# Attention with a bias on one core: V landed straight into its ring of 24 heads, late K landed side by side, joined output stores, five output tiles, 24 exponentials on VectorE

## The chip, the core and the metric

The kernel runs on one NeuronCore of a Trainium2 chip. Five engines work side by side, each in the order of its own queue: TensorE (PE, with its weight loads shown as PEld), ScalarE (ACT), VectorE (DVE), GpSimd (POOL) and SyncE (SP). Here SP issues plain DMAs only, and POOL issues only the DMAs that change float32 to bfloat16 on the way, with a one-element copy now and then (tile `tick`) that makes POOL wait until an earlier load has landed. The metric is the device time of one execution in microseconds (us). Before the change it is 231.16 us, the median of three runs (231.0 to 231.25). A change of more than 0.2% (0.46 us) is taken as told from none.

## What is computed

Four batches of eight heads, 1024 queries and 1024 keys of 64 numbers, and one bias of 1024 x 1024 that all 32 heads share:

```python
scores = scale * np.matmul(q, k.transpose(0, 1, 3, 2))
scores = scores + bias
scores_max = np.max(scores, axis=-1, keepdims=True)
attn = np.exp(scores - scores_max) / (np.sum(np.exp(scores - scores_max), axis=-1, keepdims=True) + 1e-8)
return np.matmul(attn, v).astype(np.float32)
```

The kernel leaves the maximum out (scores are small) and gets the sum of a row from a column of ones beside V.

## The kernel before

**Slots.** The 32 heads are 16 pairs, 0 to 15. A head has eight chunks of 128 queries, and one chunk of one head is a slot; 256 slots. A slot has 1024 x 128 scores (transposed) in one of three places in PSUM (`pl`, two banks each), its exponential in an `E` tile, and an output of 128 x 64. For each slot PE runs 16 matmuls of scores (`fill_half`, line 254), ACT one exponential over 128 x 1024 (`exp`, line 268), and PE eight matmuls of E with V (`av`, line 318). A place keeps its scores from one head to the next: the two halves of the contraction add the scores of this head and take away those of the last one, so that the bias is written (line 251) only where a place starts on a new chunk.

**Two groups.** The first seven pairs make slots 0 to 111, the other nine slots 112 to 255. In the first group the 14 heads run over chunks 0 to 2 (slots 0 to 41), then chunks 3 and 4 (42 to 69), then 5 to 7; so the bias chunks 3 and 4 and the rest of q of pairs 0 and 1 (`qrest`) are first used at slots 42 to 48. In the second group every pair takes six slots to begin with: pair 7 starts at slot 112, pair 15 at slot 160.

**Exponentials on DVE.** The slots in `PLAN`, 23 of them, have their exponential made by DVE in five instructions (`d_steps`, lines 285 to 301). 233 remain on ACT, the first of them in two halves.

**Loads.** POOL's order is fixed: bias 1 and 2, then k, q and v of the early pairs (`EARLY` = 7 pairs), among them the rests of q and the bias chunks 3 to 7 last; then from pair 7 on k, q and v of the late pairs (`load`, line 490). `issue` (line 478) puts a `tick` ahead of a load, which waits for the load that was issued four or five loads before (early) or two loads before (late, `LATE` = 2). q of the late pairs is loaded by `beside` (line 137): two DMAs, one for each head of the pair, that write runs of 64 numbers (128 bytes) so that the two heads lie side by side; it is then transposed in eight matmuls (line 191) where the other form takes sixteen (line 195). k of the late pairs takes the other form: one DMA with runs of 1024 bytes. v (`load_v`, line 167) lands the same way in one of three tiles `v16`, and DVE copies it into `vall` (line 508), a ring of 20 heads in which each run of 64 numbers has a one behind it.

**From a load to its first use.** PE transposes (tile `px`), DVE copies out (`ko`, `qo`), DVE negates late q (line 228), and SP copies halves from tile to tile (`ke`, `qe`, line 565).

**Outputs.** Seven slots share one bank of PSUM (`po`). `evac` (line 321) divides on DVE into an `ob` tile, one of three, and gives a store to `of` for each run of neighbouring chunks of one head; SP issues them (line 739), ACT the last.

**The order.** A planner in the kernel walks through its own model of the engines (costs such as `EXP`, `AV`, `ISSUE`, landing times such as `LATE_LOADS`) and emits each engine's instructions in the order that results. `TURNS` and `D_TURNS` are places where a listed candidate is taken rather than the rule's. The model decides only the order; on the chip semaphores hold an instruction until what it needs is there, and what stands behind it in its queue waits with it.

Of the kernel before, what the change touches and what calls it, by code (L numbers as in the profile page):

```python
# [9 lines left out]
BF = mybir.dt.bfloat16  # L10
# [6 lines left out]
def kernel(  # L17
# [13 lines left out]
    nc = tc.nc  # L31
    B, H, S, D = q.shape
# [15 lines left out]
    SPLIT, EARLY = 2, 7  # L48
    RING = 9
    LANDS = 5  # L50
    NE = 16
    VL = 3
    C0 = 3

    SIDE, SIDES = 3, 1
# [1 line left out]
    consts = ctx.enter_context(tc.tile_pool(name="consts", bufs=1))  # L57
    land = ctx.enter_context(tc.tile_pool(name="land", bufs=LANDS))
    side = ctx.enter_context(tc.tile_pool(name="side", bufs=SIDES))
    vland = ctx.enter_context(tc.tile_pool(name="vland", bufs=VL))  # L60
    kq = ctx.enter_context(tc.tile_pool(name="kq", bufs=RING))
    ep = ctx.enter_context(tc.tile_pool(name="ep", bufs=NE))
    op = ctx.enter_context(tc.tile_pool(name="op", bufs=3))
    dp = ctx.enter_context(tc.tile_pool(name="dp", bufs=2))
    dy = ctx.enter_context(tc.tile_pool(name="dy", bufs=3))
    de = ctx.enter_context(tc.tile_pool(name="de", bufs=2))
# [14 lines left out]
    zeros = ep.tile([P, NCH, P], BF, name="E")[:, :4].rearrange("p c q -> p (c q)")  # L81
    braw = consts.tile([P, NCH, S], BF)

    VR = 20
    vall = consts.tile([P, VR, NCH, D1], BF)

    b0f = dp.tile([P, S], F32, name="df")
# [35 lines left out]
    for s, x in enumerate(slots):  # L123
# [2 lines left out]


    dslots = set()
    PLAN = (46, 52, 56, 73, 84, 87, 97, 107, 120, 128, 137, 149, 160, 167, 170, 182, 188, 194, 208, 214, 226,
            230, 240)  # L130

    raws, lands, arrs = {}, {}, {}


    BESIDE = (0,)

    def beside(pr, x):

# [26 lines left out]
        return braw[:1, c, S - 1:]  # L165

    def load_v(pr):
        lands[pr, "v"] = vland.tile([P, 2, NCH, D], BF, name="v16")
        nc.gpsimd.dma_start(out=lands[pr, "v"].rearrange("p t c d -> p t (c d)"),  # L169
                            in_=vf[pr].rearrange("p t c d -> p t (c d)"))  # L170
        return lands[pr, "v"][:1, 1, NCH - 1, D - 1:]

    def arrays(pr):
        if pr not in arrs:
# [134 lines left out]
    def av(group, b, tag):  # L309
# [6 lines left out]
        for kc in range(NCH):  # L316
            for i, s in enumerate(group):
                nc.tensor.matmul(po[:, j + i, :], etile[s][:, kc, :], vall[:, slots[s][2] % VR, kc, :],  # L318
                                 start=j + i + kc == 0, stop=kc == NCH - 1, skip_group_check=True)

    def evac(b):

        po, units = bank[b]
        n = len(units)
        rs = small.tile([P, 7, 1], F32, name="rs")
        nc.vector.reciprocal(rs[:, :n, :], po[:, :n, D:D1])  # L326
        ob = olast if n == 1 else op.tile([P, 7, D], F32, name="ob")
        nc.vector.tensor_tensor(ob[:, :n, :], po[:, :n, :D], rs[:, :n, :].to_broadcast([P, n, D]), op=ALU.mult)  # L328
        stores = []

        j = 0
        while j < n:
            x, c, h, start = slots[units[j]]
            i = j + 1
            while i < n and slots[units[i]][1:3] == (c + i - j, h):
                i += 1
            stores.append((of[:, h, c:c + i - j, :], ob[:, j:i, :]))
            j = i
        return stores

    with tc.manual_schedule():

# [54 lines left out]
        double(0, 1, 0, NCH, 1, nc.vector)  # L397
        double(0, 0, 0, C0, 1, nc.vector)

        FILL, BIAS, AV = 452, 500, 264  # L400
        L_PE, L_FILL, L_ACT, L_DVE = 195, 256, 265, 140
        EXP = 904
        ISSUE, COPY = 70, 7000
        T0 = 8600.0
        bias_at = {0: T0, 1: T0, 2: 9600}
        raw_at = {(1, 1, 0): 10800, (1, 0, 0): 11500, (2, 1, 0): 12700, (2, 0, 0): 14300}
        v_at, vland_at = {}, {0: 16300}
        t_dma = 15500
        DUE = (78, 86, 137, 98, 82, 97, 114, 84, 144)
        t_pe, t_act, t_dve, t_pool = 9300.0, 9900.0, 9600.0, 9000  # L410
        filled, used = {0: T0}, {0: 9900 + L_ACT}
        av_done = {}
        e_at = {0: used[0]}
        x_free = {"xa": T0, "xb": T0}
# [37 lines left out]
        DEP = 115  # L452
        MARGIN = 160
        VSLACK = 800
        WINDOW = 4

        side_q = [x[:3] for x in pieces if SIDE <= x[0] < EARLY and x[2] == 0]
        side_open, side_at = [], {}
# [19 lines left out]
        def issue(at, cost, depth, load, pr, *a):  # L478

            nonlocal t_dma  # L480
            if 0 < depth <= len(flight):
                what, t = flight[-depth]
                nc.gpsimd.tensor_copy(tick[:], what)  # L483
                at = max(at, t + 100)
            at = pool(at, 750)
            t_dma = max(t_dma + cost, at + 2200 + cost)
            flight.append((load(pr, *a), t_dma + 200))
            return t_dma + 200
# [8 lines left out]
        def next_v(t):  # L497

            while loads_v and not any(x[2] // 2 == loads_v[0] - VR // 2 and y not in av_done for y, x in enumerate(slots)):
                if loads_v[0] - VL not in v_at:  # L500
                    break
                p = loads_v.pop(0)
                vland_at[p] = issue(t, 1600, LATE + (p > 12), load_v, p) + 2000
                move_v(p)

        def move_v(pr):
            def run(t2):
                nc.vector.tensor_copy(vall[:, 2 * pr % VR:2 * pr % VR + 2, :, :D], lands[pr, "v"][:])
                v_at[pr] = t2 + 430 + L_DVE
                next_v(v_at[pr])  # L510
            dve_q.append((vland_at[pr] + VSLACK * (pr >= EARLY), 0.3, 430, run))


        def early(kind, pr):
            nonlocal t_dma
# [207 lines left out]
        def pool(at, cost=0):  # L723
            nonlocal t_pool
            t_pool = max(t_pool, at) + cost
            return t_pool
# [49 lines left out]
        def pe_pick():  # L776
            c = pe_cands()
            if not c:
                return None
            if done_pe in TURNS:  # L780
                c.sort(key=lambda x: (x[0], x[3], x[4]))
                return c[TURNS[done_pe] % len(c)]
            fills = [x for x in c if x[3] == 0]
            others = [x for x in c if x[3] != 0]
            if others and NE <= next_act < len(acts) and acts[next_act - NE] not in av_done:

                return min(others, key=lambda x: (x[3] != 1, x[0]))
            now = [x for x in fills if x[0] <= t_pe]
            if now:


                short = len([s for s in avq[:NE] if s in e_at]) > NE - 3
                due = [x for x in others if x[3] in ((0.5, 1) if short else (0.5,)) and x[0] <= t_pe]
                if due and act_free() - FILL - L_FILL - MARGIN > t_pe + due[0][1]:
                    return due[0]
                return min(now, key=lambda x: x[4])

            limit = 1e12
            r = [y for y in (fill_ready(z[0]) for z in queue.values() if z and z[0] <= next_fill + WINDOW) if y is not None]
            if r:  # L800
                limit = max(min(r), act_free() - FILL - L_FILL - MARGIN)
            ok = [x for x in others if x[0] + x[1] <= limit]
            return min(ok + fills, key=lambda x: (x[0], x[3])) if ok + fills else None

        def dve_pick():
# [10 lines left out]
            if best[1] >= 3:  # L816
                soon = [x for x in can if x[1] < 3 and x[0] < start + 350]
                if soon:
# [1 line left out]
            return best  # L820

        done_pe, done_dve = 0, 0
        TURNS = {9: 2, 15: 0, 25: 1, 30: 0, 49: 2, 63: 2, 64: 0, 74: 1, 93: 0, 94: 0, 98: 0, 105: 0, 109: 0,
# [3 lines left out]
        D_TURNS = {1: 0, 25: 0, 34: 1, 39: 2, 41: 1, 42: 1, 44: 1, 66: 0, 68: 0, 70: 1, 71: 0, 76: 1, 81: 1,  # L827
                   82: 0, 83: 0, 88: 1, 91: 1, 107: 1, 125: 2, 128: 1, 162: 1, 165: 0, 166: 0, 171: 2, 176: 1,
                   184: 1, 195: 0, 199: 1, 201: 1, 203: 1, 204: 1, 208: 2, 211: 2, 212: 1, 222: 0}

        move_v(0)
        for x in ("k3", "q3", "v1", "k4", "q4", "v2", "k5", "q5", "v3", "k6", "q6", "v4") + tuple(LATE_LOADS):
# [75 lines left out]
```

## Time and profile before

| | before |
|---|---|
| median of three runs | 231.16 us |
| the profiled execution | 231.17 us |
| its span on the core | 229.2 us |
| granted TensorE clock, mean | 0.995 |
| GpSimd busy | 65.1 us |
| software DMA queue (POOL's loads), 30336 packets | 14.06 MB |
| hardware DMA queue (SP's copies and stores), 26560 packets | 14.40 MB |
| output stores | 158 |

The span goes from the first to the last instruction of the core; about 2 us of the time lie outside it. Busy time is the union of an engine's instructions. In a row of the timeline stand the start, the length, the engine, line, operation and tiles, and in brackets how long the engine was idle before it and what ended that. In a row of a DMA queue the share is the time that its packets took, over the time of all 16 DMA engines; an engine with two packets under way at once can bring it over 100%.

### The profile page before, as it was taken

Reading aid. Unit: us, or ns where it says so; the run is one execution under the profiler, and the core shown is the slowest. Engines: PE = TensorE matmul, PEld = TensorE weight load, DVE = VectorE, ACT = ScalarE, POOL = GpSimd, SP = SyncE. Lnnn points to the kernel's source line nnn. Section 1 sums busy time; section 2 is a strip of 40 time slices with the busy share of each in tenths; the row PEclk is TensorE's granted clock in tenths of the full one; section 3 lists DMA queues with packets and bytes.
Section 4 is the critical chain, followed back from the end, with each engine's and each line's share of the span. In section 5 each row is a group of like instructions: output and inputs, shape, how many; then the busy total and the mean of one; then the engine's idle time right before and its main releaser. Section 6 shows DMA issues by size and latency. Waiting matters only on the chain.

```text
span 229.2 us, 10571 instructions
## 1 busy us (share of the span) xinstructions
PE 219.4 (96%) x4607; PEld 208.8 (91%) x4607; DVE 197.0 (86%) x301; ACT 218.1 (95%) x238; POOL 65.1 (28%) x115
## 2 busy tenths in 40 slices
PE   7899989999999999999999999999999999899992
PEld 2789989999999999999899999999999999899991
DVE  2578878629977999999999999999999999999952
ACT  3699999999999999999999999999999999999992
POOL 8816466256455443443224310000000000000000
PEclk9999999999999999999999999999999999999998
DMA  6999999989999999999899994111121102311122
GB/s 195 216 204 215 227 227 186 223 118 110 135 113 179 169 159 184 179 97 178 207 163 243 169 238 113 49 43 43 43 50 39 44 9 66 82 50 40 34 77 75
DMA packets 57373, 29.75 MB, mean 130 GB/s; under 512 B 34864, under 2 KB 53680, under 8 KB 57328
## 3 DMA queue, kind: packets, MB, share of 16 engines
q0 software_dynamic: 30336, 14.06, 49.3%
q1 hardware_dynamic: 26560, 14.40, 23.2%
q8 instruction: 36, 0.59, 1.1%
q10 hardware_dynamic: 432, 0.62, 0.9%
q14 instruction: 9, 0.07, 0.1%
HBM read 29.36 MB, written 8.39 MB: 165 GB/s over the span
## 4 chain that ended last, share of the span: by engine, by line
PE 54%; ACT 14%; DVE 12%; issue 7%; DMA 5%; SPq 5%; DVEq 0%; ACTq 0%
PE pl L254 31%; PE po L318 16%; ACT E L268 14%; SPq L739 5%; DMA out_dram<-ob 3%; PE px L191 3%; PE pl L251 2%; PE px L195 2%; DVE dy L285 2%; DMA df<-in_k_dram 2%; DVE ob L328 2%; DVE df L296 1%; DVE de L301 1%; DVE ko L203 1%; DVE side L222 1%
## 5 line engine op out<-in xcount | busy, mean ns | idle before, releaser
L268 ACT ACTIVATE E<-pl 128x1024 bf16<-128x1024 f32 (+1 forms) x234 | 215.0, 1094 | 2.3 <-PE pl L254 2.0
L318 PE MATMUL po<-vall,E 128*128 128x65 bf16 x1864 | 86.2, 194 | 1.1 <-DVE qo L205 0.4
L254 PE MATMUL pl<-qo,ko 128*128 128x128 bf16 x1024 | 77.0, 219 | 1.2 <-ACT E L268 0.6
L318 PEld LDWEIGHTS <-E 128*128 128x128 bf16 x1864 | 74.0, 98 | 2.0 <-DVE ob L328 0.6
L254 PEld LDWEIGHTS <-ko 128*128 128x128 bf16 x1160 | 69.4, 98 | 4.3 <-issue 1.4
L254 PE MATMUL pl<-qe,ke 128*128 128x128 bf16 x888 | 65.4, 219 | 0.9 <-ACT E L268 0.3
L254 PEld LDWEIGHTS <-ke 128*128 128x128 bf16 x888 | 53.2, 98 | 2.6 <-issue 0.7
L285 DVE TENSOR_SCALAR dy<-pl 128x1024 int32<-128x1024 f32 x23 | 28.0, 1218 | 1.8 <-PE pl L254 1.7
L301 DVE SCALAR_TENSOR_TENSOR de<-dy,df 128x1024 uint16<-128x1024 int32 x23 | 27.9, 1219 | 0.7 <-PE po L318 0.4
L296 DVE SCALAR_TENSOR_TENSOR df<-df 128x1024 f32<-128x1024 f32 x23 | 28.0, 1217 | 0.1
L293 DVE SCALAR_TENSOR_TENSOR df<-df 128x1024 f32<-128x1024 f32 x23 | 27.9, 1217 | 0.1
L328 DVE TENSOR_TENSOR ob<-po,rs 128x448 f32<-128x448 f32 (+4 forms) x40 | 23.3, 583 | 2.6 <-DMA out_dram<-ob 1.1
L142 POOL DMA_DIRECT2D q<-in_q_dram x18 | 16.3, 907 | 4.4 <-PE pl L254 2.7
L326 DVE RECIPROCAL rs<-po 128x7 f32<-128x7 f32 (+5 forms) x41 | 7.9, 192 | 9.9 <-PE po L318 9.8
L290 DVE TENSOR_SCALAR df<-dy 128x1024 f32<-128x1024 uint16 x23 | 15.8, 687 | 0.3
L483 POOL COPY tick<-q 1x1 bf16<-1x1 bf16 x12 | 4.4, 367 | 33.4 <-DMA q<-in_q_dram 33.4
L203 DVE COPY ko<-px 128x1024 bf16<-128x1024 bf16 (+1 forms) x16 | 10.7, 668 | 3.3 <-PE px L195 2.5
L205 DVE TENSOR_SCALAR qo<-px,sgn 128x1024 bf16<-128x1024 bf16 (+2 forms) x18 | 12.3, 683 | 1.2 <-PE px L191 1.0
L169 POOL DMA_DIRECT2D v<-in_v_dram x16 | 11.3, 707 | 2.0 <-DVE df L296 0.3
L251 PE MATMUL pl<-ident,braw 128*128 128x128 bf16 x136 | 11.3, 226 | 0.0
L149 POOL DMA_DIRECT2D k<-in_k_dram x15 | 10.7, 711 | 2.1 <-issue 0.8
L251 PEld LDWEIGHTS <-braw 128*128 128x128 bf16 x136 | 9.9, 148 | 0.0
(58 smaller groups left out, 125.4 us busy)
## 6 DMA issues: line engine op xcount, KB each, us to landing
v<-in_v_dram POOLq DMA_DIRECT2D x16, 256.0 KB, 6.6
k<-in_k_dram POOLq DMA_DIRECT2D x15, 256.0 KB, 5.5
out_dram<-ob SPq DMA_DIRECT2D x33, 96.0 KB, 3.9
out_dram<-ob SPq DMA_DIRECT2D x92, 32.0 KB, 2.6
ke<-ko SPq DMA_DIRECT2D x22, 128.0 KB, 5.5
q<-in_q_dram POOLq DMA_DIRECT2D x18, 128.0 KB, 4.7
qe<-q SPq DMA_DIRECT2D x17, 128.0 KB, 5.0
out_dram<-ob SPq DMA_DIRECT2D x31, 64.0 KB, 2.7
```

Source lines behind the costliest of these rows:

```text
L142: nc.gpsimd.dma_start(out=t[:, :, y, :], in_=(qf, kf)[x][pr][:, y].rearrange("p (c d) -> p c d", d=D))
L203: nc.vector.tensor_copy(t["ko"][:, cs, :], px[:])
L251: nc.tensor.matmul(to, braw[:, c, :].rearrange("p (kp kc) -> p kc kp", kc=NCH)[:, kc, :], ident8[:], start=i == 0, stop=False, skip_group_ ...
L254: nc.tensor.matmul(to, kk[:, kc, :], qq[:, c, :], start=False, stop=True, skip_group_check=True)
L268: nc.scalar.activation(e[:, i:i + n].rearrange("p b x -> p (b x)"), places[slots[s][0]][:, i:i + n].rearrange("p b x -> p (b x)"), ACTF.Ex ...
L285: w.tensor_scalar(t["y"][:], places[slots[s][0]].rearrange("p b x -> p (b x)"), scale * LOG2E * 65536.0, 127.0 * 65536.0, op0=ALU.mult, op ...
L290: w.tensor_scalar(t["f"][:], t["lo"], GU / 65536.0, None, op0=ALU.mult)
L293: w.scalar_tensor_tensor(t["f"][:], t["f"][:], GP, t["f"][:], op0=ALU.add, op1=ALU.mult)
L296: w.scalar_tensor_tensor(t["f"][:], t["f"][:], GQ, t["f"][:], op0=ALU.add, op1=ALU.mult)
L301: w.scalar_tensor_tensor(etile[s].bitcast(U16).rearrange("p c q -> p (c q)"), t["y"][:], 1.0 / 512.0, t["f"][:], op0=ALU.mult, op1=ALU.add)
L318: nc.tensor.matmul(po[:, j + i, :], etile[s][:, kc, :], vall[:, slots[s][2] % VR, kc, :], start=j + i + kc == 0, stop=kc == NCH - 1, skip_ ...
L328: nc.vector.tensor_tensor(ob[:, :n, :], po[:, :n, :D], rs[:, :n, :].to_broadcast([P, n, D]), op=ALU.mult)
```

## The change

- **V in place.** `load_v` writes into `vall` itself, one DMA for each head of the pair, with runs of 64 numbers. The copy on DVE and the `v16` tiles are gone. `vall` has 24 heads in place of 20.
- **Late k side by side.** `BESIDE = (0, 1)`: k of pairs 7 to 15 is loaded as late q is, by two DMAs, and transposed in eight matmuls.
- **Stores joined.** `joined` also puts into one store the same chunk of heads at an equal distance, and takes the longest run first. Five `ob` tiles in place of three.
- **24 DVE slots** in `PLAN`, at other places; 15 `E` tiles in place of 16.
- **The planner**: other model costs (`BIAS` 530, `ISSUE` 420, 1450 for POOL's issue of v and of late q), `GRACE` = 16 (an AV group or a transpose may end 16 ns past its limit), other `DUE`, and empty `TURNS` and `D_TURNS`. A load of v no longer waits for a copy of an earlier one.

```diff
-    NE = 16
-    VL = 3
+    NE = 15
-    op = ctx.enter_context(tc.tile_pool(name="op", bufs=3))
+    op = ctx.enter_context(tc.tile_pool(name="op", bufs=5))
-    VR = 20
+    VR = 24
-    PLAN = (46, 52, 56, 73, 84, 87, 97, 107, 120, 128, 137, 149, 160, 167, 170, 182, 188, 194, 208, 214, 226,
-            230, 240)
+    PLAN = (24, 44, 50, 60, 75, 80, 90, 102, 104, 117, 136, 153, 159, 161, 169, 183, 189, 191, 198, 212, 218,
+            223, 229, 246)
-    BESIDE = (0,)
+    BESIDE = (0, 1)
     def load_v(pr):
-        lands[pr, "v"] = vland.tile([P, 2, NCH, D], BF, name="v16")
-        nc.gpsimd.dma_start(out=lands[pr, "v"].rearrange("p t c d -> p t (c d)"),
-                            in_=vf[pr].rearrange("p t c d -> p t (c d)"))
-        return lands[pr, "v"][:1, 1, NCH - 1, D - 1:]
+        for t in range(2):
+            nc.gpsimd.dma_start(out=vall[:, (2 * pr + t) % VR, :, :D], in_=vf[pr][:, t])
+        return vall[:1, (2 * pr + 1) % VR, NCH - 1, D - 1:D]
+    def joined(units):
+        out, left = [], list(range(len(units)))
+        while left:
+            best = left[:1]
+            for j in left[1:]:
+                run, dj = [left[0], j], j - left[0]
+                dc, dh = (units[j][i] - units[left[0]][i] for i in range(2))
+                if min(dc, dh) < 0 or dc and dh:
+                    continue
+                while run[-1] + dj in left and units[run[-1] + dj] == (units[run[-1]][0] + dc, units[run[-1]][1] + dh):
+                    run.append(run[-1] + dj)
+                best = max(best, run, key=len)
...
-        stores = []
...
+        return [(to, ob[:, js]) for to, js in joined([slots[u][1:3] for u in units])]
-        FILL, BIAS, AV = 452, 500, 264
+        FILL, BIAS, AV = 452, 530, 264
-        ISSUE, COPY = 70, 7000
+        ISSUE, COPY = 420, 7000
-        DUE = (78, 86, 137, 98, 82, 97, 114, 84, 144)
-        t_pe, t_act, t_dve, t_pool = 9300.0, 9900.0, 9600.0, 9000
+        DUE = (63, 123, 126, 134, 73, 76, 102, 62, 96)
+        t_pe, t_act, t_dve, t_pool = 9050.0, 9740.0, 9600.0, 9000
-        WINDOW = 4
+        WINDOW, GRACE = 4, 16
-            at = pool(at, 750)
+            at = pool(at, 1450 if load is load_v or load is load_q and pr >= EARLY else 750)
             while loads_v and not any(x[2] // 2 == loads_v[0] - VR // 2 and y not in av_done for y, x in enumerate(slots)):
-                if loads_v[0] - VL not in v_at:
-                    break
         def move_v(pr):
-            def run(t2):
-                nc.vector.tensor_copy(vall[:, 2 * pr % VR:2 * pr % VR + 2, :, :D], lands[pr, "v"][:])
-                v_at[pr] = t2 + 430 + L_DVE
-                next_v(v_at[pr])
-            dve_q.append((vland_at[pr] + VSLACK * (pr >= EARLY), 0.3, 430, run))
+            v_at[pr] = vland_at[pr] + VSLACK * (pr >= EARLY) + 300
-            ok = [x for x in others if x[0] + x[1] <= limit]
+            ok = [x for x in others if x[0] + x[1] <= limit + GRACE]
-        TURNS = {9: 2, 15: 0, 25: 1, 30: 0, 49: 2, 63: 2, 64: 0, 74: 1, 93: 0, 94: 0, 98: 0, 105: 0, 109: 0,
...
+        TURNS = {}
+        D_TURNS = {}
```

More of the change, by code (lines that the diff above doesn't have):

```diff
@@ L59 @@
     side = ctx.enter_context(tc.tile_pool(name="side", bufs=SIDES))
-    vland = ctx.enter_context(tc.tile_pool(name="vland", bufs=VL))
     kq = ctx.enter_context(tc.tile_pool(name="kq", bufs=RING))
     ep = ctx.enter_context(tc.tile_pool(name="ep", bufs=NE))
-    op = ctx.enter_context(tc.tile_pool(name="op", bufs=3))
+    op = ctx.enter_context(tc.tile_pool(name="op", bufs=5))
     dp = ctx.enter_context(tc.tile_pool(name="dp", bufs=2))
@@ L319, in av @@
                                  start=j + i + kc == 0, stop=kc == NCH - 1, skip_group_check=True)
+    def joined(units):
[10 more added lines that the diff above has]
+                best = max(best, run, key=len)
+            left = [j for j in left if j not in best]
+            (c, h), (c1, h1) = units[best[0]], units[best[-1]]
+            k = len(best) - 1
+            to = of[:, h, c:c1 + 1:max(1, (c1 - c) // max(1, k)), :] if h == h1 else of[:, h:h1 + 1:(h1 - h) // k, c, :]
+            out.append((to, slice(best[0], best[-1] + 1, best[1] - best[0] if k else 1)))
+        return out
     def evac(b):
@@ L328, in evac @@
         nc.vector.tensor_tensor(ob[:, :n, :], po[:, :n, :D], rs[:, :n, :].to_broadcast([P, n, D]), op=ALU.mult)
-        stores = []
[L331 to L339, printed above, removed]
+        return [(to, ob[:, js]) for to, js in joined([slots[u][1:3] for u in units])]
     with tc.manual_schedule():
@@ L408 @@
         t_dma = 15500
-        DUE = (78, 86, 137, 98, 82, 97, 114, 84, 144)
-        t_pe, t_act, t_dve, t_pool = 9300.0, 9900.0, 9600.0, 9000
-        filled, used = {0: T0}, {0: 9900 + L_ACT}
+        DUE = (63, 123, 126, 134, 73, 76, 102, 62, 96)
+        t_pe, t_act, t_dve, t_pool = 9050.0, 9740.0, 9600.0, 9000
+        filled, used = {0: T0}, {0: 9740 + L_ACT}
         av_done = {}
@@ L822 @@
         done_pe, done_dve = 0, 0
-        TURNS = {9: 2, 15: 0, 25: 1, 30: 0, 49: 2, 63: 2, 64: 0, 74: 1, 93: 0, 94: 0, 98: 0, 105: 0, 109: 0,
[3 rows of a table removed]
-        D_TURNS = {1: 0, 25: 0, 34: 1, 39: 2, 41: 1, 42: 1, 44: 1, 66: 0, 68: 0, 70: 1, 71: 0, 76: 1, 81: 1,
-                   82: 0, 83: 0, 88: 1, 91: 1, 107: 1, 125: 2, 128: 1, 162: 1, 165: 0, 166: 0, 171: 2, 176: 1,
-                   184: 1, 195: 0, 199: 1, 201: 1, 203: 1, 204: 1, 208: 2, 211: 2, 212: 1, 222: 0}
+        TURNS = {}
+        D_TURNS = {}
         move_v(0)
```

3 rows, old and new, of the table TURNS are left out of this document.

## The prediction

> **What bounds the kernel now.** First the page's head: its span and busy times.
>
> ```profile
> span 229.2 us, 10571 instructions
> ...
> PE 219.4 (96%) x4607; PEld 208.8 (91%) x4607; DVE 197.0 (86%) x301; ACT 218.1 (95%) x238; POOL 65.1 (28%) x115
> ```
>
> Two engines look full. The groups by line and shape tell them apart, and give the prices of the operations that the change touches:
>
> ```profile
> L268 ACT ACTIVATE E<-pl 128x1024 bf16<-128x1024 f32 x232 | 213.9, 1098 | 1.0 <-PE pl L254 0.7
> L301 DVE SCALAR_TENSOR_TENSOR de<-dy,df 128x1024 uint16<-128x1024 int32 x23 | 27.9, 1219 | 0.7 <-PE po L318 0.4
> L290 DVE TENSOR_SCALAR df<-dy 128x1024 f32<-128x1024 uint16 x23 | 15.8, 687 | 0.3
> L195 PE MATMUL px<-ident,k 128*64 128x128 bf16 x176 | 7.0, 222 | 0.0
> L508 DVE COPY vall<-v 128x1024 bf16<-128x1024 bf16 x16 | 6.9, 433 | 0.8 <-DMA v<-in_v_dram 0.8
> L328 DVE TENSOR_TENSOR ob<-po,rs 128x128 f32<-128x128 f32 x1 | 0.3, 292 | 1.1 <-DMA out_dram<-ob 1.1
> ```
>
> ACT sets the time: 232 exponentials are back to back, 213.9/232 = 0.92 us each, with 1.0 us idle before all of them together. PE has to keep pace: any wait in PE's queue longer than the slot or so by which it is ahead (about 1.0 us) becomes ACT's idle time. So I ask what feeds PE: the loads. The windows, whose last two columns are the DMA share and GB/s, show two regimes:
>
> ```profile
> 30.00:40.00 10.00, 9.36 (x187) 8.68 (x185) 8.15 (x20) 9.67 (x12) 6.33 (x15) 1.00 1.17 209
> 140.00:150.00 10.00, 9.95 (x223) 9.75 (x221) 9.77 (x14) 10.00 (x12) 0.00 (x0) 1.00 0.23 61
> ```
>
> While POOL loads, the DMA engines are full (1.17); afterwards they are nearly free (0.23).
>
> **The change part by part. One exponential less on ACT**: -0.92 us. DVE gets four steps of about 1.22 us and one of 0.69 = 5.6 us, and loses 16 copies of 0.433 = 6.9 us; at 86% busy it has the room, so I take nothing (without that room the worst is the 5.6 us of one chain, and only if it falls on a stretch where DVE decides).
>
> **Tail.** The last instructions of all engines, in order:
>
> ```profile
> 221.67 3.03 ACT L268 ACTIVATE E<-pl 128x1024 bf16<-128x1024 f32 x3
> 224.75 0.43 PE L318 MATMUL po<-vall,E 128*128 128x65 bf16 x8 [0.33 <-ACT E L268]
> 225.69 0.29 DVE L328 TENSOR_TENSOR ob<-po,rs 128x128 f32<-128x128 f32 x1 [1.06 <-DMA out_dram<-ob]
> 225.90 0.16 DVE L326 RECIPROCAL rs<-po 128x1 f32<-128x1 f32 x1
> 226.46 0.41 ACTq L739 DMA_DIRECT2D out_dram<-olast  x1
> ```
>
> The last bank's division at 225.90 stood behind a DVE instruction that waited 1.06 us for an `ob` tile whose store hadn't landed. With five tiles the wait goes; the division then follows its matmuls (225.18 and some 0.1 to 0.2 for the result), so 0.5 to 0.7 comes off: -0.6. Fewer stores help the same wait and get nothing of their own. Bounds: 0 to -1.06.
>
> **K's transposes**: eight matmuls instead of sixteen, nine times. At best 72 of them at the 7.0/176 = 0.04 us by which they follow each other, 2.9 us of PE's 219.4; but PE waits for ACT, so 0 for the end. `GRACE` (16 ns) and the model's constants move order alone: 0 to 16 ns a time. Taking out `TURNS` may cost a stall or save one; ACT idles only 1.0 us now, so there is little to win; 0 taken, +2 at worst.
>
> **V in place, late k side by side: the DMA side.** Both turn loads of one DMA with 256 runs into two with 1024 runs each. Late q has had this form all along, so its price stands in the trace. Four windows: 9 to 46 us (hardly any but long-run loads), 46 to 72 (late k and q in turn), one pair of late q almost alone (50.4 to 53.4), and the densest stretch (57.4 to 58.6).
>
> ```profile
> q0 software_dynamic: 6310, 6.32, 105.6%
> ```
> ```profile
> q0 software_dynamic: 8584, 2.05, 87.1%
> ...
> k<-in_k_dram POOLq DMA_DIRECT2D x4, 256.0 KB, 4.7
> q<-in_q_dram POOLq DMA_DIRECT2D x8, 128.0 KB, 4.6
> ```
> ```profile
> q0 software_dynamic: 2072, 0.28, 152.4%
> ```
> ```profile
> q0 software_dynamic: 1061, 0.13, 175.1%
> ```
>
> A long-run load: 6310 packets are 24.6 loads of 256, in 37 us: 1.50 us each, at a full queue. A short-run pair (2048 packets): 3.0 us in the third window. At the peak 1061 took 1.2 us: 2.3 us a pair. Their time there, 1.75 x 1.2 = 2.1 us of all 16 engines for 1061, is 4.06 for a pair; were the engines held to the 105.6% of the first window, 3.85 us. So a load that changes form costs 0.8 to 2.35 us more of a full queue; I take 1.15, nearer the low end, because in the dense stretches two short packets were plainly under way per engine (175%). Sixteen v and nine k: 25 times.
>
> The Trainium skill (DMA: Bandwidth & Descriptors, Specifications) puts the least transfer for line rate at 512 bytes; 128-byte runs lie below it, and the third window's 0.28 MB in 3.0 us against the first's 6.32 MB in 37 agrees, at 0.09 against 0.17 MB per us.
>
> **Where that lands, early.** POOL's ticks show when loads land, PE's row when pair 1's rest of q is used, a row of the chain of waits where ACT's full exponentials begin (9.78), SP's when pair 15 is complete.
>
> ```profile
> 7.19 0.75 POOL L169 DMA_DIRECT2D v<-in_v_dram  x1
> ...
> 39.49 0.18 POOL L483 COPY tick<-qrest 1x1 bf16<-1x1 bf16 x1 [0.91 <-DMA qrest<-in_q_dram]
> ...
> 46.93 0.71 POOL L149 DMA_DIRECT2D k<-in_k_dram  x1 [0.29 <-issue]
> 48.65 1.79 POOL L142 DMA_DIRECT2D q<-in_q_dram  x2 [0.29 <-PE pl L254]
> ...
> 54.18 1.24 POOL L483 COPY tick<-q 1x1 bf16<-1x1 bf16 x1 [2.10 <-DMA q<-in_q_dram]
> ...
> 124.61 1.74 POOL L142 DMA_DIRECT2D q<-in_q_dram  x2 [0.20 <-DMA qe<-q]
> ...
> 133.28 0.38 POOL L483 COPY tick<-q 1x1 bf16<-1x1 bf16 x1 [4.76 <-DMA q<-in_q_dram]
> ```
> ```profile
> 43.40 0.47 PE L195 MATMUL px<-ident,qrest 128*64 128x128 bf16 x10
> ```
> ```profile
> 9.78 4.69 ACT E L268 x5
> ```
> ```profile
> 138.29 0.47 SPq L565 DMA_DIRECT2D qe<-q  x1
> ```
> ```profile
> qe<-q SPq DMA_DIRECT2D x1, 128.0 KB, 2.6
> ```
>
> Seven v's (pairs 0 to 6, the first at 7.19) stand ahead of pair 1's rest of q, which landed at 39.4 and was used at 43.4. After the change it is 7 x 1.15 = 8.05 us later, 47.4, and so are the bias chunks behind it. The need is 0.92 us earlier, for slot 24 is now DVE's: 42.5. PE stands 4.9 us late; less its lead of 1.0: **ACT +4.0 us**. Behind that transpose stand all fills. At 0.8 per v it is 5.6 - 3.1 - 1.0 = 1.5; at 2.35, 16.5 - 4.1 = 12.4; at 0.6, nothing. V itself is ready 0.43 us sooner once landed, as its copy is gone, and POOL's issue grows from 0.7 to 1.8 us a load: 25 more of 1.1 us, hidden under its ticks, since four or five loads are under way. Without that cover a load would cost the 1.1 us, about what I count for the queue anyway, not on top of it. The AV matmuls now wait for the DMA itself, and what stands behind them on PE is fills, on which ACT waits: the same 4.0 us, not more. With 15 E tiles ACT may run one slot (0.92 us) less far ahead of AV; its 1.0 us of idle time is put down to PE's scores, so I take 0, and 0.92 once at worst. The wider ring frees v of pair 12 on when pair 0's last slot (75) is through, at 9.8 + 71 x 0.92 = 75 us, before POOL gets there. Fewer stores ahead of them can only bring SP's `ke` and `qe` copies sooner; 0.
>
> **Late.** Late loads begin 8.05 later, 46.9 to 55.0. Pair 15's q was issued as the 24th late load (nine k, nine q, six v), so a load took (124.61 - 46.93)/23 = 3.38 us. That pace is set by the tick two loads back: landing over two. With every load of q's form it lies between half of q's quickest (48.65 to 54.18: 2.8) and half of its slowest here (124.61 to 133.28, and the tick: 4.5). I take 3.4, today's, though the long-run loads are gone. Now v of pair n-1 always comes after q of pair n, so q of pair 15 is 25th: issued at 55.0 + 24 x 3.4 = 136.6, landed 7.0 later (between 5.5 and 8.7): 143.6. Today it lands at 133.2, its last copy at 138.29 + 2.6 = 140.9, and ACT reaches slot 160 at 9.8 (slot 1) + 148 x 0.92 = 146 (12 of the 160 before it are DVE's); PE fills a place some 1.0 ahead, so about 4.0 of slack: needed by 137.2, moved by +4.0 - 0.92 to 140.3. **ACT +3.3 us** (0 at a pace of 2.8; some 30 at 4.5).
>
> **Sum**: 229.2 - 0.92 - 0.6 + 4.0 + 3.3 = 235.0 of span; the profiled execution's 231.17 less 229.2 is 2.0 outside it, and its time agrees with the median of the runs: 237.0 us.
>
> **The rivals.** *The loads keep up* (the other side): short-run packets stay at the peak's two per engine with a longer queue behind them than late q ever had, so a v costs 0.6 more or less, under the 4.1 us of early slack over seven; and late loads run at 3.0 or quicker. For it: 175%. Against it: even the pair that ran alone took 3.0 us. The two gains remain: 229.2 - 1.5 + 2.0 = 229.7. It decides at 4.1/7 = 0.59 us per v. The Trainium skill (the same page, Anatomy of one DMA) counts 2.0 us plus bytes over 436 GB/s, so the form would change nothing and this rival would hold; the trace speaks against it, as 128 KB at that rate is 0.3 us and the densest 1061 packets took 1.2.
>
> *One stretch alone is late*: 229.7 + 4.0 or + 3.3, 233 to 234.
>
> *The order decides*: loads keep up, but the plan without `TURNS` lets PE come late here and there, +1 to +2: 230.7 to 231.7. For it: 1.0 us of idle today shows a very close order. Against it: PE and DVE both get lighter.
>
> *The change doesn't do what it says for PE*: k's transposes are halved but their waits stay; 0 either way, it changes no time here.
>
> **How the numbers follow.** Both stretches late 0.50, one alone 0.18, loads keep up 0.24, order 0.08. The likeliest gives 237.0. Its own range runs from 232 (1.5 and 0.8 late) to 250 (12.4 and a pace of 3.6). The range for 8 in 10 reaches down into the rival that keeps up, 229.5, and up to 247, where the dearer half of the DMA bounds is left out. Faster by over 0.2% (0.46 us; less can't be told from none): the rival that keeps up and a little of the order, 0.26; within it 0.05; slower 0.69.
>
> **What would show it.** Right: the software queue holds 30336 + 25 x 1792 = 75,000 packets and is full from 9 us past 50; ACT idle of several us near 43 to 50, released by PE, PE by `qrest` or `braw`; last load past 145; ticks on v as long as those on q. The tail's wait for `ob` gone. Wrong: the rest of q still landing by 43, the last v landing near 140, or ACT's idle time below 2 us. If DVE's or SP's rows end ACT's waits, the step on loads was wrong.

## The result and the profile after

The changed kernel takes 242.82 us (median of four runs, 241.94 to 243.9), the kernel before 231.2 us beside it: a ratio of 1.0495 [1.0441, 1.0549], 11.6 us slower. The forecast was 237.0. Now and then an execution lies over 1.5% above the quickest of its kernel; the ratios to the kernel before and their 95% intervals, in brackets here and below, leave it out, the medians don't. The profiled execution took 241.94 us; from its page come the span, the busy times, and two rows of the 40 slices (6 us each).

```profile
span 240.0 us, 10460 instructions
...
PE 219.1 (91%) x4535; PEld 210.2 (88%) x4535; DVE 196.8 (82%) x292; ACT 216.7 (90%) x237; POOL 91.2 (38%) x140
...
ACT  3104999999999999999999999899999999999993
PEclk9657999999999999999999999999999999999999
```

ACT works 1.4 us less than before, PE, PEld and DVE within 1.4 us of what they did; POOL's 26 us more are issues of loads. The time is idle time, and the row of ACT shows nearly all of it in one place: slices 2 to 4 of 40. The timeline of ACT, whole from its first exponential to its last store:

```profile
21.01 0.60 ACT L265 ACTIVATE E<-pl 128x512 bf16<-128x512 f32 x1 [13.54 <-PE pl L251]
22.08 62.27 ACT L265 ACTIVATE E<-pl 128x512 bf16<-128x512 f32 x68 [0.47 <-PE pl L251]
84.69 67.02 ACT L265 ACTIVATE E<-pl 128x1024 bf16<-128x1024 f32 x73 [0.34 <-PE pl L251]
152.58 83.80 ACT L265 ACTIVATE E<-pl 128x1024 bf16<-128x1024 f32 x91 [0.87 <-PE pl L251]
237.46 0.34 ACTq L739 DMA_DIRECT2D out_dram<-olast  x1
```

And the first exponential of the kernel before, in the same view:

```profile
8.22 0.60 ACT L268 ACTIVATE E<-pl 128x512 bf16<-128x512 f32 x1 [0.79 <-PE pl L254]
```

So the span divides in three. To the first exponential: 21.01 against 8.22, **+12.8**. From there to the end of the last: 236.38 - 21.01 = 215.4 against 224.70 - 8.22 = 216.5, **-1.1**, with only 0.47, 0.34 and 0.87 us of idle time on the way. From there to the issue of the last store: 1.1 against 1.8, **-0.7**. Their sum, 11.0, agrees with the 10.8 us between the spans. The stretches near 43 to 50 and past 120, where I had put the loss, show no more than the 0.87.

What ACT waited for at the start stands in the waits (us in all, times, longest) and in the timeline of all engines:

```profile
DVE vall L380 <- DMA vall<-in_v_dram: 15.4, 1, 15.4
ACT E L265 <- PE pl L251: 15.2, 4, 13.5
PE px L188 <- DVE de L383: 13.2, 1, 13.2
POOL vall L167 <- DVE vall L380: 6.8, 1, 6.8
```
```profile
7.19 1.75 POOL L167 DMA_DIRECT2D vall<-in_v_dram  x2
...
16.69 0.22 DVE L380 MEMSET vall<- 128x192 bf16 x1 [15.40 <-DMA vall<-in_v_dram]
...
17.70 0.58 DVE L383 CAST de<-dy 128x384 bf16<-128x384 f32 x1
```

Read from the bottom up: ACT waits for scores, PE for the cast of the first q (line 383), and that cast stands on DVE behind a fill of 0.22 us, the ones beside V (line 380). The fill is emitted behind `load_v(0)`. That load used to write `v16`; now it writes `vall`, in other columns (0 to 63; the ones are column 64), but the same tile, and a semaphore holds the fill until v of pair 0 has landed. The same tie runs the other way too: POOL's next load of v waited 6.8 us for the fill.

### The profile page after: what moved, and what is told of

Its sections match the earlier page's. It is cut to its first block, busy times and chain, and to the rows that moved or that the text cites. A ratio compares the mean times of both kernels' runs of the same rounds, so it can differ in the third digit from the quotient of the medians.

```text
span 240.0 us, 10460 instructions
## 1 busy us (share of the span) xinstructions
PE 219.1 (91%) x4535; PEld 210.2 (88%) x4535; DVE 196.8 (82%) x292; ACT 216.7 (90%) x237; POOL 91.2 (38%) x140
## 3 DMA queue, kind: packets, MB, share of 16 engines
q0 software_dynamic: 75536, 14.06, 72.0%
## 4 chain that ended last, share of the span: by engine, by line
PE 50%; ACT 19%; issue 10%; DVE 10%; DMA 6%; POOL 3%; SPq 1%; DVEq 0%; ACTq 0%; POOLq 0%
PE pl L251 29%; ACT E L265 19%; PE po L315 12%; PE px L188 4%; DMA vall<-in_v_dram 3%; PE pl L248 3%; DMA out_dram<-ob 2%; DVE ob L345 2%; DVE dy L282 2%; DVE de L298 1%; DVE df L290 1%; PE px L192 1%; SPq L739 1%; DVE df L293 1%; DVE df L287 1%
## 5 line engine op out<-in xcount | busy, mean ns | idle before, releaser
L265 ACT ACTIVATE E<-pl 128x1024 bf16<-128x1024 f32 (+1 forms) x233 | 213.5, 1104 | 15.4 <-PE pl L251 15.2
L315 PE MATMUL po<-vall,E 128*128 128x65 bf16 x1856 | 87.4, 194 | 1.0 <-DVE rs L343 0.5
L282 DVE TENSOR_SCALAR dy<-pl 128x1024 int32<-128x1024 f32 x24 | 29.3, 1220 | 7.5 <-PE pl L251 6.8
L167 POOL DMA_DIRECT2D vall<-in_v_dram x32 | 29.3, 922 | 8.7 <-DVE vall L380 6.8
L290 DVE SCALAR_TENSOR_TENSOR df<-df 128x1024 f32<-128x1024 f32 x24 | 29.3, 1219 | 0.2
L293 DVE SCALAR_TENSOR_TENSOR df<-df 128x1024 f32<-128x1024 f32 x24 | 29.2, 1218 | 0.1
L298 DVE SCALAR_TENSOR_TENSOR de<-dy,df 128x1024 uint16<-128x1024 int32 x24 | 29.1, 1217 | 0.1
L287 DVE TENSOR_SCALAR df<-dy 128x1024 f32<-128x1024 uint16 x24 | 16.8, 702 | 0.1
L140 POOL DMA_DIRECT2D k<-in_k_dram x18 | 15.9, 887 | 1.7 <-PE pl L251 1.2
L202 DVE TENSOR_SCALAR qo<-px,sgn 128x1024 bf16<-128x1024 bf16 (+2 forms) x18 | 12.3, 684 | 1.3 <-PE px L188 1.2
L188 PEld LDWEIGHTS <-de 128*128 128x128 bf16 x11 | 1.1, 136 | 13.8 <-DVE de L383 13.7
L188 PE MATMUL px<-ident,de 128*128 128x128 bf16 x7 | 0.9, 306 | 13.2 <-DVE de L383 13.2
L380 DVE MEMSET vall<- 128x192 bf16 x1 | 0.2, 218 | 15.4 <-DMA vall<-in_v_dram 15.4
```

What stands on the lines that cost most here:

```text
L140: nc.gpsimd.dma_start(out=t[:, :, y, :], in_=(qf, kf)[x][pr][:, y].rearrange("p (c d) -> p c d", d=D))
L167: nc.gpsimd.dma_start(out=vall[:, (2 * pr + t) % VR, :, :D], in_=vf[pr][:, t])
L265: nc.scalar.activation(e[:, i:i + n].rearrange("p b x -> p (b x)"), places[slots[s][0]][:, i:i + n].rearrange("p b x -> p (b x)"), ACTF.Ex ...
L282: w.tensor_scalar(t["y"][:], places[slots[s][0]].rearrange("p b x -> p (b x)"), scale * LOG2E * 65536.0, 127.0 * 65536.0, op0=ALU.mult, op ...
L287: w.tensor_scalar(t["f"][:], t["lo"], GU / 65536.0, None, op0=ALU.mult)
L290: w.scalar_tensor_tensor(t["f"][:], t["f"][:], GP, t["f"][:], op0=ALU.add, op1=ALU.mult)
```

## The experiments

Two theories stood after this. **W**: the start's wait is the whole loss, the loads cost nothing. **L**: the short-run loads cost several us, as forecast, but hide under the late start. POOL's timeline speaks for L:

```profile
45.30 0.28 POOL L490 COPY tick<-qrest 1x1 bf16<-1x1 bf16 x1
...
52.07 1.94 POOL L140 DMA_DIRECT2D k<-in_k_dram  x2 [0.35 <-PE pl L251]
...
137.64 1.92 POOL L140 DMA_DIRECT2D q<-in_q_dram  x2 [0.74 <-DMA ke<-ko]
...
141.91 1.92 POOL L167 DMA_DIRECT2D vall<-in_v_dram  x2 [0.28 <-issue]
```

Pair 1's rest of q is ticked off at 45.3, 5.8 us later than before, and pair 15's q is issued at 137.6, 13.0 later; a kernel that starts on time would have been kept waiting by that.

### 1. The fill moved ahead of the loads

```diff
+        nc.vector.memset(vall[:, :, :, D:D1], 1.0)
         for c in (1, 2):
             load_b(c)
...
-        nc.vector.memset(vall[:, :, :, D:D1], 1.0)
```

> Theory W (a wait at the start): in the changed kernel the fill of vall's ones column on VectorE stands behind the landing of pair 0's v (15.4 us idle), and ACT's first exponential is at 21.01 us instead of 8.22. With the fill put ahead of the loads ACT starts at 8.2 to 8.5 again and the whole 12.8 us go: span 240.0 - 12.8 = 227.2, time about 229.2, 0.8% under the kernel before, and ACT's idle time inside the stretch stays under 2 us. Theory L (loads, the forecast's): the late start only hid that loads are late. POOL's queue is released 6.8 us sooner, but its loads at 3.57 us each still bring pair 15's q to about 141 to 143 us, where ACT needs it by 136.3; ACT then idles 5 to 7 us between 140 and 155, time 234 to 236.

240.1 us (237.67 to 241.86), 1.0306 [1.0214, 1.0397]. W's 229.2 fell; L's 234 to 236 was too low. The timeline of ACT, shortened to its gaps:

```profile
7.87 0.60 ACT L265 ACTIVATE E<-pl 128x512 bf16<-128x512 f32 x1 [0.71 <-PE pl L251]
...
41.08 3.77 ACT L265 ACTIVATE E<-pl 128x1024 bf16<-128x1024 f32 x4 [0.80 <-PE pl L251]
45.67 2.85 ACT L265 ACTIVATE E<-pl 128x1024 bf16<-128x1024 f32 x3 [0.83 <-PE pl L251]
48.83 1.97 ACT L265 ACTIVATE E<-pl 128x1024 bf16<-128x1024 f32 x2 [0.30 <-PE pl L251]
51.17 23.14 ACT L265 ACTIVATE E<-pl 128x1024 bf16<-128x1024 f32 x25 [0.37 <-PE pl L251]
...
124.49 1.02 ACT L265 ACTIVATE E<-pl 128x1024 bf16<-128x1024 f32 x1 [3.91 <-PE pl L251]
125.95 1.02 ACT L265 ACTIVATE E<-pl 128x1024 bf16<-128x1024 f32 x1 [0.43 <-PE pl L251]
128.02 4.69 ACT L265 ACTIVATE E<-pl 128x1024 bf16<-128x1024 f32 x5 [1.04 <-PE pl L251]
135.14 1.02 ACT L265 ACTIVATE E<-pl 128x1024 bf16<-128x1024 f32 x1 [2.43 <-PE pl L251]
136.35 19.36 ACT L265 ACTIVATE E<-pl 128x1024 bf16<-128x1024 f32 x21 [0.19 <-PE pl L251]
```

The start is back at 7.87. ACT idles at 41 to 51, in the early stretch that the prediction named, and at 120 to 136, ahead of the 146 at which the prediction had ACT reach pair 15 and of L's 140 to 155. The waits name the loads:

```profile
ACT E L265 <- PE pl L251: 12.3, 14, 3.9
...
PE px L188 <- DMA k<-in_k_dram: 4.0, 1, 4.0
...
PEld L192 <- DMA qrest<-in_q_dram: 2.3, 2, 1.4
```

### 2. The wait alone, put into the kernel before

A copy of one element of pair 0's landed v on DVE, ahead of the same fill:

```diff
+        nc.vector.tensor_copy(wait0[:], lands[0, "v"][:1, 1, NCH - 1, D - 1:])
         nc.vector.memset(vall[:, :, :, D:D1], 1.0)
```

> The kernel before with one thing added: VectorE copies one element of pair 0's landed v ahead of the fill of the ones column, so that it waits as the changed kernel does, with no other part of the change. Theory W: ACT's first exponential moves from 8.2 to about 21, time 231.2 + 12 to 13 = 243 to 244. If start-up could take in a part of the wait, less: under 240. Theory L has no part in it, as the loads are those of the kernel before.

244.61 us (two runs; W said 243 to 244), 1.0539 [1.0479, 1.0599]. The waits and ACT's timeline:

```profile
POOL v L170 <- DVE vall L510: 13.4, 3, 8.4
DVE wait L374 <- DMA v<-in_v_dram: 13.4, 1, 13.4
```
```profile
19.56 0.60 ACT L269 ACTIVATE E<-pl 128x512 bf16<-128x512 f32 x1 [12.29 <-PE pl L255]
```

A wait of this kind is enough for a loss of 12 us in a kernel whose k and v are loaded in long runs (here later loads of v waited too, 13.4 us, for DVE's copies, which stood behind it). So each cause alone makes a loss, the loads 7.9 us (experiment 1) and the wait 12.4, against 232.25 for the kernel before beside them; they have to be separated by taking the loads' price away.

### 3 and 4. Loads of the same bytes in long runs, order kept

The kernel of experiment 1, every engine's order kept; first v's DMAs alone, then late k's too, write runs of 1024 bytes. The values then stand in wrong places, and VectorE makes one more fill, of seven columns, at the start. That takes the short packets away and the longer issue on POOL with them (1.05 us for two DMAs, 1.74 before), so both are in the price.

```diff
-            nc.gpsimd.dma_start(out=vall[:, (2 * pr + t) % VR, :, :D], in_=vf[pr][:, t])
+            nc.gpsimd.dma_start(out=vall[:, (2 * pr + t) % VR].rearrange("p c d -> p (c d)")[:, :NCH * D],
+                                in_=vf[pr][:, t].rearrange("p c d -> p (c d)"))
...
+            if x:
+                nc.gpsimd.dma_start(out=t.rearrange("p c t d -> p (c t d)")[:, y * NCH * D:(y + 1) * NCH * D], in_=kf[pr][:, y])
+                continue
```

> e1 with every instruction of PE, ACT, VectorE and SP in e1's order, and POOL's loads in e1's order; only v's DMAs write runs of 1024 bytes (512 numbers on end into the ring, so its values stand in the wrong places and the output is not the reference's; VectorE also fills seven columns once). Theory L: v's price goes without any change of order. Pair 1's rest of q lands at 39 to 41 instead of 44.5, pair 15's q at 134 to 140 instead of 149, most of ACT's 12 us of idle time goes: 231 to 233.5. Rival O (the order or 15 E tiles): stays at 236 or more.

> e8 with late k's DMAs in runs of 1024 bytes too (two DMAs still, its values in wrong places, output not the reference's), order as in e1. Theory L: all loads as cheap as in the kernel before, so this is the rival of the forecast in which the loads keep up: 229 to 230.5, pair 15's q lands by 134. Rival O: 233 or more.

v alone: 231.37 us, 0.9928 [0.9892, 0.9965], as L had it. v and k: 228.42 us (228.12 to 228.69), 0.9839 [0.9808, 0.987], just under L's 229 to 230.5. The software queue, first of experiment 1, then of this one (packets, MB, share of the 16 engines):

```profile
q0 software_dynamic: 75536, 14.06, 73.0%
```
```profile
q0 software_dynamic: 30736, 14.06, 50.0%
```

The waits of the second:

```profile
ACT E L269 <- PE pl L255: 1.9, 4, 0.7
```

The same bytes in 44,800 fewer packets are 11.7 us quicker by the medians, 10.8 by the ratios (0.0467 x 232.0, the median of the kernel before beside them): 8.8 for v and 2.1 for k by the ratios. ACT's wait for scores falls from 12.3 to 1.9 us, 10.4 of them. This is the price of the short runs, their longer issue included, and 228.42 is what the rest of the change is worth without it: with copies gone and nothing late, 3.6 us below the kernel before. How the price divides between packets and issue no run shows. GpSimd spends 44.4 us on issuing v and late k in experiment 1 and 27.3 here, and still waits longer there in its ticks for k, q and v to land, 41.2 us against 33.8: the landings came later too.

### 5. Long runs with the wait at the start left in

Experiment 4 with the fill back behind the loads:

```diff
-        nc.vector.memset(vall[:, :, :, D:D1], 1.0)
         for c in (1, 2):
...
+        nc.vector.memset(vall[:, :, :, D:D1], 1.0)
```

> The changed kernel itself, with its wait at the start, and v and late k in runs of 1024 bytes as in e9 (values in wrong places, output not the reference's). Theory that the two causes hide each other: the start's 12 to 13 us stay and the loads were not waited for anyway, so e9 + 12: 241 to 243, the changed kernel's 242.8 within 1.5. Rival, that they add up: it falls by e1's 9 us to about 233 to 235.

240.21 us, 1.0367 [1.0324, 1.0409], just under the 241 to 243 expected and far from the 233 to 235 of causes that add up; the waits and ACT's first exponential:

```profile
DVE vall L385 <- DMA vall<-in_v_dram: 14.1, 1, 14.1
```
```profile
19.82 0.60 ACT L269 ACTIVATE E<-pl 128x512 bf16<-128x512 f32 x1 [12.45 <-PE pl L255]
```

This closes the square. With neither cause 228.4; the short runs alone 240.1; the wait alone 240.2; both, the changed kernel, 242.8. Each costs nearly 12 us by itself (10.8 and 12.2 by the ratios), and the second adds only some 2.6 to the first (3.0 to 4.4 by the ratios): a kernel that starts 12.8 us late needs its loads 12.8 us later, and the loads don't start later by as much (the first late k leaves at 52.07 in the changed kernel, at 51.32 in experiment 1).

### 6. Three output tiles, and stores joined in the kernel before

Experiment 1 with `bufs=3` for `ob`; and the kernel before with `joined` in `evac`, whose planner still counts the stores that fell away, so that the order of its engines stays:

```diff
-    op = ctx.enter_context(tc.tile_pool(name="op", bufs=5))
+    op = ctx.enter_context(tc.tile_pool(name="op", bufs=3))
```
```diff
-        return stores
+        new = [(to, ob[:, js]) for to, js in joined([slots[u][1:3] for u in units])]
+        return [None] * (len(stores) - len(new)) + new
```

> e1 with three output tiles instead of five. The forecast's tail term: the last evacuation waits for a store again, 0.5 to 0.7 us between ACT's last exponential and the last store's issue come back: e1 + 0.6. Rival: the joined stores alone had freed the tiles in time, e1 + 0 to 0.1.

> The kernel before with the joined stores alone (three output tiles; PE, VectorE, ACT and POOL in the same order). Tail: the wait of the last evacuation for a store (1.06 us) goes or shrinks, 0.4 to 0.7 us less between ACT's last exponential and the last store: 230.5 to 230.8, ratio 0.997. Rival: stores across heads land later (runs of 256 bytes) and nothing is won, 231.0 to 231.4.

Three tiles: 239.5 us, 1.0307 [1.0259, 1.0355], as with five (1.0306). Joined alone: 231.68 us, 0.9994 [0.9972, 1.0017], no change. Neither the 0.6 us expected back with three tiles nor the 0.4 to 0.7 expected off with joined stores shows, though these times scatter by as much. The ends in the timelines tell more, first with three tiles (one execution, of 244.45 us, the longest of four), then the kernel before with stores joined (one of 233.46, the longest of twelve):

```profile
238.90 0.43 PE L315 MATMUL po<-vall,E 128*128 128x65 bf16 x8 [0.39 <-ACT E L265]
...
240.00 0.34 ACTq L739 DMA_DIRECT2D out_dram<-olast  x1
```
```profile
226.41 0.43 PE L318 MATMUL po<-vall,E 128*128 128x65 bf16 x8 [0.38 <-ACT E L268]
228.02 0.29 DVE L348 TENSOR_TENSOR ob<-po,rs 128x128 f32<-128x128 f32 x1 [1.78 <-DMA out_dram<-ob]
```

With three tiles the end takes 1.10 us from the last matmuls to the last issue, and no division waits for `ob`. With joined stores in the old order it waits 1.78 us. So, by these two executions, the end is shorter than the 1.71 us of before (224.75 to 226.46) neither for the tiles nor for the joined stores alone. That leaves the new order, with the joined stores or without them; the two weren't tried apart.

### 7. Ways that keep the output: fewer short loads

Late k in one long run (`BESIDE = (0,)`); v through `v16` and a copy on DVE as before (ring of 20, four output tiles, k side by side); both; and real load costs in the planner. All start from experiment 1. The core of the fourth, which also tells the planner the measured landing times of the early loads and POOL's longer issue of late k:

```diff
-            raw_at[pr, 1, 0] = issue(t, 1600, LATE, load_k, pr) + LATER
+            raw_at[pr, 1, 0] = issue(t, 3000, LATE, load_k, pr) + LATER
-                vland_at[p] = issue(t, 1600, LATE + (p > 12), load_v, p) + 2000
+                vland_at[p] = issue(t, 3000, LATE + (p > 12), load_v, p) + 2000
-                vland_at[pr] = issue(0, E1, depth, load_v, pr)
+                vland_at[pr] = issue(0, 2300, depth, load_v, pr)
```

> e1 with late k in long runs again (nine loads of one DMA). Theory L: nine loads take 0.8 to 1.15 us less each, pair 15's q lands 7 to 10 us sooner than in e1 and the idle time near 150 goes: 229.5 to 231, at least 3 us under e1. Theory W: no load is waited for, so it is e1 within 0.5 us, perhaps 0.3 slower for sixteen transposes a pair.

> e1 with v landed as in the kernel before: one DMA in long runs into one of three tiles, copied by VectorE into a ring of 20 heads (four output tiles, which is what the memory then has room for). Late k stays side by side, 24 slots, joined stores, new plan. Theory L: early loads are on time again (pair 1's rest of q lands at 39 to 40, not 44.5), the late ones start at 47 and take 3.2 to 3.4 us each, pair 15's q lands at 131 to 137: 229.7 to 231.5. Rival: the rest of the change (order without the listed turns, k side by side) is what costs; still 233 or more.

> e6 with late k in long runs too: of the change only the joined stores, the 24 slots, 15 E tiles, the planner's constants and the empty lists of turns are left. Theory L: all loads as before the change: 229.7 to 231.0, and pair 15's q lands 2 to 6 us sooner than in e6 without a gain in time. Rival: those parts cost by themselves, over 232.

> e1 (ones first) with the planner's model told what loads cost in e1's trace: 3.0 us of DMA for late k and v, 2.3 for early v, 1.45 of POOL for late k, and the landing times of the last early loads as e1 showed them. The loads are the same, only the order of PE, VectorE and SP changes. Theory L (the loads themselves bind): pair 15's q lands at 146 to 149 as in e1, against 136.3 needed, so the idle time only moves together, late: e1 - 2 to e1 + 1, 238 to 241. Rival O (the order binds: PE is put to wait for loads that nobody needs yet): the idle time goes for the most part, 231 to 234.

In that order: 241.35 us, 1.0414 [1.0348, 1.0479]; 233.26 us, 1.005 [1.0008, 1.0093]; 237.97 us, 1.0252 [1.0188, 1.0316]; 252.37 us, 1.0847 [1.0751, 1.0942]. Only the second gained clearly, 6.8 us on experiment 1 (5.9 by the ratios), and none came out as L had it (229.5 to 231.5 for the first three, 238 to 241 for the fourth). Long runs for k are worth 2.1 us where the order is kept, yet these kernels are 1.3 (within the scatter) and 4.7 slower with them (241.35 against 240.1, 237.97 against 233.26). Another form of load changes the planner's times, and with them the order of every engine, and PE transposes late k in sixteen matmuls again. In the third kernel every load has the form of the kernel before and the start is late by 1.0 us only (first exponential at 9.19); it still takes 237.97, with ACT waiting 10.2 us for scores at 13 places: there it is not the loads' form that costs. With real costs in the planner it is worst; two gaps of ACT's timeline there:

```profile
152.96 4.69 ACT L265 ACTIVATE E<-pl 128x1024 bf16<-128x1024 f32 x5 [7.24 <-PE pl L251]
164.92 1.02 ACT L265 ACTIVATE E<-pl 128x1024 bf16<-128x1024 f32 x1 [7.28 <-PE pl L251]
```

`PLAN` and `DUE` were left as they are in these four; whether lists made for the new costs would give the time back wasn't tried. These runs say nothing exact about loads, since more than one thing changes at once; that is why experiments 3 and 4 keep the order.

### 8. Long runs, and GpSimd puts them in place

v and late k land in runs of 1024 bytes in two shared tiles, and GpSimd copies them to where they belong, the order of the other engines kept; three output tiles.

```diff
+            moves.append(lambda: nc.gpsimd.tensor_copy(to.rearrange("p c t d -> p t c d"), t[:]))
...
+        moves.append(lambda: nc.gpsimd.tensor_copy(vall[:, x:x + 2, :, :D], t[:]))
```

> A version meant to keep the change and drop its price, with the reference's output: e1's order on PE, ACT, VectorE and SP, v and late k landed by one DMA in runs of 1024 bytes into two tiles, and GpSimd copying v into the ring and late k side by side, in the places where its ticks stood (three output tiles, for room). 25 issues of 1.8 us become 0.7, and 25 copies come in; the trace has no such copy, the nearest row is GpSimd's fill of 64x1024 in 0.95 us, so 1 to 2 us each. Theory L: loads as cheap as in e9 but 1 to 2 us later at their use: 228.5 to 230.5, under the kernel before by 0.6 to 1.5%. Rival: GpSimd's copies hold up the loads behind them in its queue, over 3.5 us a load again and pair 15's q after 140: 233 or more.

235.58 us (234.03 to 238.51), 1.0126 [1.0073, 1.0178]: 7.2 below the changed kernel, above the kernel before (232.16), and some 5 us above what L expected. It came out as the rival's 233 or more, though pair 15's q left at 133.18, not after 140. From the groups by line, GpSimd's and VectorE's (busy us, mean ns; the profiled execution took 238.51 us, the longest of six):

```profile
L189 POOL COPY vall<-v 128x1024 bf16<-128x1024 bf16 x16 | 19.0, 1186 | 18.2 <-DMA v<-in_v_dram 18.1
...
L164 POOL COPY k<-v 128x1024 bf16<-128x1024 bf16 x9 | 10.6, 1174 | 3.1 <-DMA v<-in_k_dram 3.1
```
```profile
L306 DVE TENSOR_SCALAR dy<-pl 128x1024 int32<-128x1024 f32 x24 | 29.2, 1219 | 4.8 <-PE pl L275 4.8
L317 DVE SCALAR_TENSOR_TENSOR df<-df 128x1024 f32<-128x1024 f32 x24 | 31.8, 1325 | 0.1
```

POOL waits 18.1 us for loads with its copies, and while it waits it issues none. ACT waits 8.8 us for scores at 16 places. None of the versions tried keeps the output and beats the kernel before.

## Why the prediction was right, and where it was wrong

**Slower, by the loads: right as a mechanism.** Changing 25 loads to short runs makes PE late and ACT idle, early and late; that is shown by experiments 1 and 4, which differ in the loads and in one fill at the start. The packets were forecast at 75,000 (75,536). "The loads keep up", the rival at 229.7, would have been right with long runs (228.4) and was wrong with these. The Trainium skill (DMA: Bandwidth & Descriptors, Anatomy of one DMA) counts a fixed 2.0 us and the bytes of a DMA; these two kernels move the same 14.06 MB in as many DMAs some 11 us apart, so that sum misses the difference. Its least transfer of 512 bytes for line rate (Specifications) agrees with the sign.

**Early, +4.0: too much.** In experiment 1 the gaps of 41 to 51 are 0.80 + 0.83 + 0.30 + 0.37 = 2.3 us. The mis-sized term is the price of a v. GpSimd's tick in experiment 1:

```profile
44.68 0.18 POOL L490 COPY tick<-qrest 1x1 bf16<-1x1 bf16 x1
```

Pair 1's rest of q was there at 44.7 at the latest, not at 47.4: (44.7 - 39.5)/7 = 0.74 us a v, where 1.15 was taken, and 0.8 was the low bound. With 0.74 the prediction's own sum gives 5.2 - 3.1 - 1.0 = 1.1 us. The rest of the 2.3 isn't in that sum: PE waited for pair 0's rest of q as well, and the last two gaps, 0.30 and 0.37, come while PE, its lead gone, writes the bias of new chunks; in experiment 4, in the same order, ACT has no gap there.

**Late, +3.3: too little, and at another load.** The pace was forecast at 3.4 us and measured at (137.64 - 52.07)/24 = 3.57, so pair 15's q left at 137.6 instead of 136.6; in experiment 1, without the late start, it was (141.45 - 51.32)/24 = 3.76. But I asked only when pair 15 is due. In experiment 1 ACT loses 8.0 us between 120 and 137 (3.91 + 0.43 + 1.04 + 2.43, and 0.19), and PE's longest wait there is for pair 13's k, issued at 114.08:

```profile
122.53 1.01 PE L188 MATMUL px<-ident,k 128*128 128x128 bf16 x8 [4.04 <-DMA k<-in_k_dram]
```

Every late pair has its own due time, and an earlier one was missed first.

**V in place: the step that failed.** I counted a copy less, 0.43 us sooner, and AV behind the DMA. The wait that this adds, the fill of the ones behind the first v, is not in the prediction, and it is what the profile of the changed kernel shows: 12.8 us at the start. Since this delay covers the loads', the forecast of +7.3 for late loads is hardly to be found in that profile, and two of the signs that I named, ACT idle at 43 to 50 and waits of PE for `qrest`, weren't there. The time lay in the range, 5.8 us above the forecast, and that is partly luck: what the changed kernel's profile shows as lost is lost to a wait that the sum doesn't have. The loads alone, without it, give 240.1, 3.1 above the forecast.

**One exponential less, -0.92, and the tail, -0.6: right in size.** Measured -1.1, for the whole stretch between the first exponential and the last, and -0.7. The tail's reason was wrong: not the five tiles (experiment 6).

**The order, +1 to +2:** not shown in the changed order itself, which gives 228.4 with nothing late. It is shown as a danger, and a larger one than +2: with all loads in their old form and the order planned anew, experiment 7's third kernel takes 237.97, and with the loads of experiment 1 its fourth loses 12 us (252.37 against 240.1).

## What to carry to other kernels

When a DMA is sent straight into a tile that something else also fills, list every other writer of that tile and its place in the queues, even where no byte is shared: a fill of 0.22 us held VectorE for 15.4 us. Two delays in a row hide each other, so a profile that shows one cause does not acquit the other; take each out alone, with the order of the engines kept. For a chain of loads, ask for the due time of every load, not of the last one.

## What the runs showed of the hardware

While PE stood idle at the start of the changed kernel, the granted TensorE clock fell. Windows of 10 us (start and end, length, busy times of PE, PEld, DVE, ACT and POOL, the clock, DMA share, GB/s):

```profile
10.00:20.00 10.00, 1.67 (x16) 1.58 (x17) 2.50 (x7) 0.00 (x0) 3.18 (x5) 0.50 1.31 150
20.00:30.00 10.00, 10.00 (x185) 9.17 (x183) 6.40 (x16) 8.52 (x11) 7.97 (x16) 0.92 1.41 155
```

The clock was 0.50 in the idle stretch, back at 0.92 on average over the next, and from its first exponential at 21.01 on ACT had no gap of over 0.5 us there. The Trainium skill (TensorE: Matmul & The Clock Gate, Part 1: The HAM clock gate) gives half speed for an idle array; the trace agrees. In experiment 1 PE's wait of 4.04 us was enough: from 122 to 126 the clock was 0.57, and the eight transposes behind the wait took 1.01 us, those at 126.66 took 0.62.

GpSimd's copies of 128x1024 bf16 took 1.18 us each (experiment 8), where VectorE's took 0.433 in the kernel before, and one of VectorE's steps of the exponential beside them rose from 1218 ns, in the changed kernel below, to 1325 on average. The step that reads PSUM (line 306 there) kept its 1219, 1220 in the changed kernel.

```profile
L293 DVE SCALAR_TENSOR_TENSOR df<-df 128x1024 f32<-128x1024 f32 x24 | 29.2, 1218 | 0.1
```

The Trainium skill (SBUF — State Buffer, SBUF: two separate sides) says that GpSimd and VectorE share a pair of ports, which one of them holds for a whole instruction; the longer mean agrees with it, though no run here tells this cause from another.
